# The mLSTM's gate columns inside the first group of memory queries

## The chip, the cores and the metric

The kernel runs on one core of a Trainium2 chip. The metric is the device time of one launch in microseconds, the median of several runs. One core has a matrix engine (TensorE, in the profile PE, its weight loads PEld), VectorE (DVE), ScalarE (ACT), GpSimd (POOL) and the sync engine (SP), which here only issues DMAs. Each works off its own queue of instructions in order. Products accumulate in eight PSUM banks.

## The reference

The reference is a decoder trunk of two layers for 256 tokens of width 1024. Each layer is a SwiGLU feed-forward half step, a token mixer beside memory cross-attention, and another half step. The change is in the first mixer, the mLSTM. One input matrix of 3592 columns serves all of it:

```python
proj = hn @ a_w_in[j]              # 256 tokens x 3592 columns
q, k  = tok[..., :512], tok[..., 512:1024]
v     = tok[..., 1024:2048]
o_gate = sigmoid(tok[..., 2048:3072])
gates = tok[..., 3072:3080] + gate_b
i_pre, logf = gates[..., :4], log_sigmoid(gates[..., 4:])
xq = proj[..., 3080:3592]          # memory queries, 4 heads of 128
q_mem = rms_norm(xq per head); softmax(q_mem k_mem^T / sqrt(128)) v_mem
```

`hn` is the RMS norm of the input. All is float32, and a product of float32 accuracy is made of three: each operand is split into a rounded part `h` and the rest `l`, and `h·h`, `h·l` and `l·h` are added up.

## The kernel before

Activations stand transposed: four tiles `xh` (rounded) and `xl` (rest), each 128 channels by 2 by 256 tokens. The RMS scale of a token is not applied to the input; it multiplies the results later, as a row `x.rb` (one value a token along the free axis) or as a column `x.rc` (one value a partition). Both come out of a chain that ends while the mixer's first products already run.

**Weights.** A `Stream` brings them from HBM in chunks, in a fixed `plan`. Each chunk passes a DMA into one of five `wr` buffers (`fetch`, sync queue), a rounding copy on ScalarE into `wh` (`round`) and a subtraction on VectorE into `wl` (`rest`). A chunk is copied at most `AHEAD = 5` chunks ahead of the one in use. A full chunk is 128 partitions by 4x256 and feeds 24 matmuls.

**Groups.** A `Group` is 256 output columns, two full chunks, 48 matmuls into one bank. In the usual form the weights are the stationary operand and the 256 tokens move, so the result has channels on partitions. With `rows=True` the activations are stationary and 256 weight columns move, so the result has tokens on partitions. `mm3` issues the three products; all matmuls of it are line 449 in the profile. Transposes are line 463, plain float32 products (`mmf`) line 458.

**The first mixer** (`mixer_a`) computes in this order: two groups of output gates, chunks alternating; the eight gate columns; two more groups of output gates; two groups of memory queries (`rows=True`); queries and keys; values; the output projection. The gate columns are a chunk of their own, 8x8 numbers a partition. They are spread over a tile of 128 columns, four at 0 and four at 32, after a memset of the rest on GpSimd (lines 299 and 311). Eight row chunks by three products give 24 matmuls that put the input gates on partitions 0 to 3 and the forget gates on 32 to 35 of `gate_bank`. `gates()` copies these rows out, multiplies them by `x.rb` and goes on with bias, exponential, logarithm and scans, writes a row to HBM and reads it back to all partitions.

**Consumers.** `out_gate` scales a group and, once the gates are done, applies a sigmoid (line 1025); the first loads ScalarE's sigmoid table, the last of four loads the table with exponential and logarithm again. `cross` takes a bank of memory queries through `head_norm` (squares on ScalarE, a reduction on VectorE, a power on GpSimd, a scaling), transposes the result (`turn`), and spawns two heads: scores, maximum, exponential (line 929), scaling, transposes, values.

**Order.** All instructions are put in order by a planner at build time, `Weave`. It has a clock of TensorE that grows with each matmul and a clock for each other engine, fed by estimated costs (`Job`). The main program yields every six matmuls or so; there the planner lets every chain run whose planned time has come, and fills the stream. Chains that put work on TensorE ask for `room`, a free bank.

Of the kernel before, what the change touches and what calls it, by code (L numbers as in the profile page):

```python
# [10 lines left out]
F32 = mybir.dt.float32  # L11
# [41 lines left out]
AHEAD = 5  # L53
LEAD = 0.4
NEAR = 2
HOP = 0.04
POLL = 0.6

# [54 lines left out]
class Job:  # L113
# [13 lines left out]
    def act(self, n=8, total=False):  # L127
        return self.use("act", 0.14 + n * 0.00092 + 0.09 * total)
# [12 lines left out]
def tile_trunk(ctx: ExitStack, tc: tile.TileContext, a, out):  # L141
# [3 lines left out]
    def mk(pool, shape, dt, tag):  # L145
        seq[0] += 1
        return pool.tile(shape, dt, tag=tag, name=f"{tag}_{seq[0]}")
# [121 lines left out]
    class Stream:  # L269
# [22 lines left out]

        def round(self, i):
            shape, j = self.plan[i][1], Job(wv, self.landed[i])
            gates = shape[2] == 8
            n = 1024 if gates else shape[1] * shape[2]
            self.hi[i] = mk(whp[i % 2], [P, 8, P] if gates else shape, F32R, f"wh{i % 2}")
            if gates:
                nc.gpsimd.memset(self.hi[i].bitcast(F32), 0.0)
                for s in range(2):  # L300
                    nc.scalar.copy(self.hi[i][:, :, s * 32:s * 32 + 4], self.raw[i][:, :, s * 4:s * 4 + 4])
            else:
                nc.scalar.copy(self.hi[i], self.raw[i])  # L303
            self.cast[i] = j.act(n)

        def rest(self, i):
            shape, j = self.plan[i][1], Job(wv, self.cast[i])
            gates = shape[2] == 8
            self.lo[i] = mk(wlp[i % 2], [P, 8, P] if gates else shape, F32R, f"wl{i % 2}")
            if gates:  # L310
                nc.gpsimd.memset(self.lo[i].bitcast(F32), 0.0)
                for s in range(2):
                    d = slice(s * 32, s * 32 + 4)
                    tt(out=self.lo[i][:, :, d], in0=self.raw[i][:, :, s * 4:s * 4 + 4],
                       in1=self.hi[i][:, :, d].bitcast(F32), op=ALU.subtract)
                j.dve(64)
            else:
                tt(out=self.lo[i], in0=self.raw[i], in1=self.hi[i].bitcast(F32), op=ALU.subtract)  # L318
                j.dve(shape[1] * shape[2])
            self.subbed[i] = j.t  # L320

        def fill(self):
# [42 lines left out]
    def chunks(w):  # L365
        return w.rearrange("(k p) f -> p k f", p=P)
# [54 lines left out]
    def mixer_plan(w, pair, rest, w_out, gates=None):  # L421
        for kh in range(2):
            for c0 in pair:
                yield cols(w, c0, kh)
        for c0 in rest:
            if c0 == gates:
                yield chunks(w)[:, :, c0:c0 + 8], [P, 8, 8], None
                continue
            for kh in range(2):
                yield cols(w, c0, kh)  # L430
        for kc in ORDER + LATE:
            yield row(w_out, kc)

    A_PAIR, A_REST = (2048, 2304), (3072, 2560, 2816, 3080, 3336, 0, 512, 256, 768, 1024, 1280, 1536, 1792)
    B_PAIR, B_REST = (1024, 1280), (1536, 0, 256, 512, 768)
    plan = list(mem_plan())
    for i, (src, shape, _) in enumerate(list(ffn_plan(a["ffn1_w_in"][0], a["ffn1_w_out"][0]))):
# [209 lines left out]

    def head_norm(j, dst, src, n, x, scales):

        hd = src.shape[2] // n  # L650
        sq, v, u = tmp(), col(), col()
        sqv = sq[:, :, :n * hd]
        act(sqv, src, AF.Square)
        yield j.act(2 * n * hd)
        nc.vector.tensor_reduce(out=v[:, 0:2 * n].rearrange("p (h m) -> p h m", h=2),
                                in_=sqv.rearrange("p h (m d) -> p h m d", m=n), axis=AX.X, op=ALU.add)
        j.dve(2 * n * hd)
        yield from x.wait(j)
        hsc = scales(j)
        for h in range(2):  # L660
            nc.vector.tensor_scalar(u[:, n * h:n * h + n], v[:, n * h:n * h + n], hsc[:, h:h + 1], EPS,
                                    op0=ALU.mult, op1=ALU.add)
            j.dve()
        power(j, u[:, 8:8 + 2 * n], u[:, 0:2 * n], 2 * n)
        yield j.t
        for h in range(2):
            nc.vector.tensor_scalar(v[:, 8 + n * h:8 + n * h + n], u[:, 8 + n * h:8 + n * h + n],
                                    hsc[:, 2 + h:3 + h], None, op0=ALU.mult)
            j.dve()
        tt(out=dst.rearrange("p h (m d) -> p h m d", m=n), in0=src.rearrange("p h (m d) -> p h m d", m=n),  # L670
           in1=v[:, 8:8 + 2 * n].rearrange("p (h m) -> p h m", h=2).unsqueeze(3).to_broadcast([P, 2, n, hd]),
           op=ALU.mult)
        j.dve(2 * n * hd)
# [227 lines left out]
        def has(self, *kcs):  # L901
            return lambda: all(kc in self.done for kc in kcs)

    def cross(gr, gi, layer, x, scales, ys):
        j = Job(wv)
        qn = unit(F32)
        yield from head_norm(j, qn, gr.ps, 2, x, scales)
        gr.b.free()
        yield from room(j, 1)
        b = turn(qn)  # L910
        yield j.pe()
# [96 lines left out]
    def mixer_a(x, nxt):  # L1008
# [26 lines left out]
                yield from gr.part(kh)  # L1035


        yield main_banks(1)
        gate_bank = Bank()
        yield ws.ready()  # L1040
        gh, gl = ws.take()
        for kc in range(8):
            mm3(gate_bank.t[:, :T], gh[:, kc], gl[:, kc], x.xh[kc // 2][:, kc % 2], x.xl[kc // 2][:, kc % 2],
                start=kc == 0, stop=kc == 7)
            if kc % 2 == 1:
                yield
        ws.drop()

        def gates():
            j, ps = Job(wv), gate_bank.t  # L1050
            yield from x.wait(j)
            gt = [unit(F32) for _ in range(4)]
            ipre, fpre, ab, bc, av, gg, em, one = (gt[i // 2][0:4, i % 2] for i in range(8))
            nc.vector.memset(one, 1.0)
            nc.scalar.copy(ipre, ps[0:4, :T])
            j.act(T)
            nc.scalar.copy(fpre, ps[32:36, :T])
            yield j.act(T)
            gate_bank.free()
            tt(out=ipre, in0=ipre, in1=x.rb[0:4], op=ALU.mult)  # L1060
            tt(out=fpre, in0=fpre, in1=x.rb[0:4], op=ALU.mult)
            nc.vector.tensor_scalar(ipre, ipre, gbias[:, 0:1], None, op0=ALU.add)
            nc.vector.tensor_scalar(fpre, fpre, gbias[:, 1:2], None, op0=ALU.add)
            stt(out=ab, in0=fpre, scalar=-1.0, in1=fpre, op0=ALU.mult, op1=ALU.max)
            for _ in range(6):
                j.dve(T)
            yield j.t
            act(ab, ab, AF.Exp, scale=-1.0)
            j.act(T)
            act(ab, ab, AF.Ln, bias=1.0)  # L1070
            yield j.act(T)
            stt(out=fpre, in0=fpre, scalar=0.0, in1=ab, op0=ALU.min, op1=ALU.subtract)
            nc.vector.tensor_tensor_scan(bc, one, fpre, 0.0, ALU.mult, ALU.add)
            tt(out=av, in0=ipre, in1=bc, op=ALU.subtract)
            nc.vector.tensor_tensor_scan(gg, one, av, 0.0, ALU.mult, ALU.max)
            tt(out=em, in0=bc, in1=gg, op=ALU.add)
            for _ in range(7):
                j.dve(T)
            yield j.t
            gd = a["gd"]  # L1080
            nc.gpsimd.dma_start(gd, gg)
            gb = [unit(F32) for _ in range(2)]
            for i in range(2):
                nc.gpsimd.dma_start(gb[i], gd[2 * i:2 * i + 2, :].partition_broadcast(P))
            st["gb"], st["at"] = gb, j.t + 9.0
            act(em, em, AF.Exp, scale=-1.0)
            st["gates"] = j.act(T)
            acol = mk(gp, [P, 16], F32, "acol")
            yield from room(j, 1)
            b = Bank()  # L1090
            for i, r in enumerate((av, em)):
                for h in range(2):
                    transpose(b.t[:, (2 * i + h) * 4:(2 * i + h) * 4 + 4], r[:, h * P:(h + 1) * P])
            yield j.pe()
            nc.vector.tensor_copy(acol, b.t[:, :16])
            j.dve()
            b.free()
            st["acol"], st["at"] = acol, max(st["at"], j.t)

        wv.spawn(gates())  # L1100
        for i, gr in enumerate(gs):
            wv.spawn(out_gate(i, gr))
        for i in range(2, 4):
# [1 line left out]
            gr = Group(x)  # L1105
            yield from gr.all()
            wv.spawn(out_gate(i, gr))
        hsc = head_scales(x, P, True)
        for gi in range(2):
            yield main_banks(1)  # L1110
            gr = Group(x, rows=True)
            yield from gr.all()
            wv.spawn(cross(gr, gi, 0, x, hsc, ys))

        def decay(hd):
            j = Job(wv)
# [188 lines left out]
    def mixer_b(x, nxt):  # L1305
# [130 lines left out]
            for gr in (g0, g1):  # L1436
                yield from gr.part(kh)
        wv.spawn(keys(g0))
        wv.spawn(cross(g1, 0, 1, x, hsx, ys))
        yield main_banks(1)  # L1440
        gr = Group(x, rows=True)
        yield from gr.all()
        wv.spawn(cross(gr, 1, 1, x, hsx, ys))
        for gi in range(4):
            yield main_banks(1)
            gr = Group(x, rows=True)
# [55 lines left out]
```

## Time and profile before

| | |
|---|---|
| median of 3 runs | 1001.41 us (1001.22 to 1002.0) |
| the profiled execution's own time | 1001.35 us |
| its span, first to last instruction | 999.6 us |
| instructions | 20574 |
| TensorE matmuls | 8554 |
| DMA, mean | 183 GB/s |

In the profile's groups a row names line, engine and operation, then what is written and read, the moving operand first (`bank<-xh,wh`: the activations move, the weights stand; `bank<-wh,xh`: the other way round). "x1544" is a count, then come busy time, mean duration of one and idle time before. Matmuls overlap in the pipeline: one is shown as some 280 ns long, but the next starts much sooner, so prices are read from the distance of their starts. In the chain of waits a piece is a stretch of one line's work, with start, length and count.

### The profile page before, as it was taken

To read this page: it belongs to the slowest core of one execution; us is meant where nothing else is said; L and a number is where in the kernel's file an instruction comes from. 1 tells how busy PE (TensorE), PEld (TensorE's weight loads), DVE (VectorE), ACT (ScalarE), POOL (GpSimd) and SP (SyncE) were. 2 spreads that over 40 slices of the span, in tenths; PEclk is the share of its full clock that TensorE was granted. 3 is DMA by queue.
4 is the path that set the end of the run, shared out by engine and by line. 5 is a ranking of instruction groups with operands and counts; after the bars stand their busy time and mean duration, and the time that the engine had idled before them with its cause. 6 is when DMAs were issued, how large, how long until landed. Compare 5 with 4: busy or idle time off the path is not lost.

```text
span 999.6 us, 20574 instructions
## 1 busy us (share of the span) xinstructions
PE 991.2 (99%) x8554; PEld 976.6 (98%) x8554; DVE 677.3 (68%) x1096; ACT 511.0 (51%) x774; POOL 56.7 (6%) x46
## 2 busy tenths in 40 slices
PE   8999999999999999999999999999999999999998
PEld 7999999999999999999999999999998899999997
DVE  6985675578767596666568676656678788665561
ACT  6754444356656464454454544444566765544440
POOL 1400000011001000000010000001122010000000
PEclk9999999999999999999999999999999999999999
DMA  9876656666354566655676557565623357666550
GB/s 298 246 236 208 190 168 195 208 170 201 114 172 134 183 211 203 210 180 173 197 216 195 190 170 225 187 197 174 189 85 101 98 163 252 189 193 211 187 169 23
DMA packets 171613, 182.71 MB, mean 183 GB/s; under 512 B 7196, under 2 KB 165328, under 8 KB 171520
## 3 DMA queue, kind: packets, MB, share of 16 engines
q1 hardware_dynamic: 170384, 179.60, 57.7%
q8 instruction: 67, 1.10, 0.4%
q0 software_dynamic: 416, 0.75, 0.4%
q10 hardware_dynamic: 720, 1.05, 0.3%
q14 instruction: 26, 0.21, 0.1%
HBM read 180.32 MB, written 1.05 MB: 181 GB/s over the span
## 4 chain that ended last, share of the span: by engine, by line
PE 98%; DMA 1%; ACT 0%; DVE 0%; issue 0%; SPq 0%; DVEq 0%; ACTq 0%
PE bank L449 93%; PE bank L458 2%; PE bank L463 2%; DMA wr<-in_mem_w_kv_dram 1%; PE bank L1374 1%; PE bank L1425 1%; PE bank L1369 0%; DMA u<-in_memT_dram 0%; ACT wh L303 0%; ACT u L709 0%; DVE wl L318 0%; DVE t L868 0%; DVE t L869 0%; SPq L379 0%; DVE u L711 0%
## 5 line engine op out<-in xcount | busy, mean ns | idle before, releaser
L318 DVE TENSOR_TENSOR wl<-wr,wh 128x1024 fp32r<-128x1024 f32 (+2 forms) x349 | 407.0, 1204 | 51.9 <-ACT wh L303 50.5
L449 PE MATMUL bank<-xh,wh 128*128 128x256 f32 x1544 | 427.4, 277 | 0.0
L449 PE MATMUL bank<-xh,wl 128*128 128x256 f32 x1544 | 426.4, 276 | 0.0
L449 PE MATMUL bank<-xl,wh 128*128 128x256 f32 x1544 | 426.4, 276 | 0.0
L303 ACT CAST wh<-wr 128x1024 fp32r<-128x1024 f32 (+2 forms) x349 | 339.0, 1019 | 74.4 <-PE bank L449 48.9
L449 PE MATMUL bank<-u,wh 128*128 128x256 f32 x1792 | 307.9, 277 | 0.0
L449 PEld LDWEIGHTS bank<-xh,wh 128*128 128x128 f32 x1544 | 289.8, 188 | 0.1
L449 PEld LDWEIGHTS bank<-xl,wh 128*128 128x128 f32 x1544 | 289.8, 188 | 0.1
L449 PEld LDWEIGHTS bank<-xh,wl 128*128 128x128 f32 x1544 | 289.8, 188 | 0.0
L449 PEld LDWEIGHTS bank<-u,wh 128*128 128x128 f32 x1792 | 269.8, 188 | 1.7 <-issue 1.7
L449 PE MATMUL bank<-u,wl 128*128 128x256 f32 x896 | 247.5, 276 | 0.0
L449 PEld LDWEIGHTS bank<-u,wl 128*128 128x128 f32 x896 | 168.2, 188 | 0.0
L800 ACT ACTIVATE t<-t 128x512 f32<-128x512 f32 x44 | 27.9, 633 | 185.9 <-DVE t L797 185.5
L797 DVE TENSOR_TENSOR t<-bank,rb 128x256 f32<-128x256 f32 x88 | 36.5, 422 | 77.2 <-PE bank L449 77.2
L449 PE MATMUL bank<-wh,xh 128*128 128x256 f32 x208 | 60.1, 289 | 0.0
L449 PE MATMUL bank<-wl,xh 128*128 128x256 f32 x208 | 58.1, 279 | 0.0
L449 PE MATMUL bank<-wh,xl 128*128 128x256 f32 x208 | 58.0, 279 | 0.0
L497 ACT ACTIVATE xh<-u,gcol 128x256 fp32r<-128x256 f32 x48 | 21.6, 501 | 71.2 <-DVE u L850 58.6
L523 POOL TENSOR_TENSOR u<-u,t 128x512 f32<-128x512 f32 x14 | 24.3, 1736 | 592.5 <-ACT t L520 592.4
L847 DVE TENSOR_TENSOR t<-bank,hrb 128x512 f32<-128x512 f32 x15 | 10.4, 691 | 62.1 <-PE bank L449 62.1
L803 DVE TENSOR_TENSOR t<-t,bank 128x256 f32<-128x256 f32 x88 | 33.0, 417 | 27.0 <-ACT t L800 26.9
L469 DVE TENSOR_TENSOR u<-t,u 128x512 fp32r<-128x512 f32 x44 | 30.4, 691 | 28.2 <-ACT u L467 28.2
(189 smaller groups left out, 658.9 us busy)
## 6 DMA issues: line engine op xcount, KB each, us to landing
wr<-in_ffn_w_in_dram SPq DMA_DIRECT2D x176, 512.0 KB, 5.2
wr<-in_ffn_w_out_dram SPq DMA_DIRECT2D x80, 512.0 KB, 4.9
wr<-in_a_w_in_dram SPq DMA_DIRECT2D x28, 512.0 KB, 4.7
wr<-in_b_w_in_dram SPq DMA_DIRECT2D x14, 512.0 KB, 4.7
wr<-in_a_w_out_dram SPq DMA_DIRECT2D x12, 512.0 KB, 3.9
wr<-in_b_w_out_dram SPq DMA_DIRECT2D x12, 512.0 KB, 3.3
wr<-in_ffn_w_out_dram SPq DMA_DIRECT2D x16, 256.0 KB, 2.8
wr<-in_mem_w_kv_dram SPq DMA_DIRECT2D x6, 512.0 KB, 7.6
```

The costliest lines, as they stand in the source:

```text
L303: nc.scalar.copy(self.hi[i], self.raw[i])
L318: tt(out=self.lo[i], in0=self.raw[i], in1=self.hi[i].bitcast(F32), op=ALU.subtract)
L449: nc.tensor.matmul(ps, lhsT, rhs, start=start, stop=stop, skip_group_check=True)
L458: nc.tensor.matmul(ps, lhsT, rhs, start=start, stop=stop, skip_group_check=True)
L463: nc.tensor.transpose(ps, src, ident[:k, :k])
L469: tt(out=lo, in0=src, in1=hi.bitcast(F32), op=ALU.subtract)
L497: act(hi[:, m], xn[:, m], AF.Copy, scale=g(self.gi + 2 * c2 + m))
L523: nc.gpsimd.tensor_tensor(out=self.acc, in0=self.acc, in1=sq, op=ALU.add)
L797: tt(out=t[:, m], in0=bs[m].t[:, :T], in1=x.rb, op=ALU.mult)
L800: act(t, t, AF.Silu)
L803: tt(out=t[:, m], in0=t[:, m], in1=bs[m].t[:, T:], op=ALU.mult)
L847: tt(out=t, in0=halves(b.t), in1=pair(x.hrb), op=ALU.mult)
```

## The change

The eight gate columns lie next to the first 256 columns of the memory queries in the input matrix. They are now one stretch of 264 columns. Its chunks are 2 row chunks by 264 columns, four of them, and the group is placed where the gates stood, behind the first two groups of output gates. It has the rows' form, one bank for each half of the tokens: 48 matmuls of 264 moving columns. The gates come out with tokens on partitions. `gates()` copies their eight columns of each half out, scaled by `x.rc`, into a zeroed tile of 36 columns (four at 0, four at 32), and two transposes bring them into the old layout; the multiplications by `x.rb` are gone. The memory queries are the columns 8 to 263 of both banks. `head_norm` and `cross` take a list of two such views, and work on the halves one after the other. The second query group follows the output gates as before, and so do all others.

```diff
+GATED = 264
...
         def round(self, i):
             shape, j = self.plan[i][1], Job(wv, self.landed[i])
-            gates = shape[2] == 8
-            n = 1024 if gates else shape[1] * shape[2]
-            self.hi[i] = mk(whp[i % 2], [P, 8, P] if gates else shape, F32R, f"wh{i % 2}")
-            if gates:
-                nc.gpsimd.memset(self.hi[i].bitcast(F32), 0.0)
-                for s in range(2):
-                    nc.scalar.copy(self.hi[i][:, :, s * 32:s * 32 + 4], self.raw[i][:, :, s * 4:s * 4 + 4])
-            else:
-                nc.scalar.copy(self.hi[i], self.raw[i])
-            self.cast[i] = j.act(n)
+            self.hi[i] = self.split(whp[i % 2], f"wh{i % 2}", shape)
+            nc.scalar.copy(self.hi[i], self.raw[i])
+            self.cast[i] = j.act(shape[1] * shape[2])
+
+        def split(self, pool, tag, shape):
+            if shape[2] == GATED:
+                return mk(pool, [P, shape[1], 384], F32R, tag)[:, :, :GATED]
+            return mk(pool, shape, F32R, tag)
...
             if c0 == gates:
-                yield chunks(w)[:, :, c0:c0 + 8], [P, 8, 8], None
+                for k in range(0, 8, 2):
+                    yield chunks(w)[:, k:k + 2, c0:c0 + GATED], [P, 2, GATED], None
                 continue
...
-    A_PAIR, A_REST = (2048, 2304), (3072, 2560, 2816, 3080, 3336, 0, 512, 256, 768, 1024, 1280, 1536, 1792)
+    A_PAIR, A_REST = (2048, 2304), (3072, 2560, 2816, 3336, 0, 512, 256, 768, 1024, 1280, 1536, 1792)
...
-        yield main_banks(1)
-        gate_bank = Bank()
-        yield ws.ready()
-        gh, gl = ws.take()
-        for kc in range(8):
-            mm3(gate_bank.t[:, :T], gh[:, kc], gl[:, kc], x.xh[kc // 2][:, kc % 2], x.xl[kc // 2][:, kc % 2],
-                start=kc == 0, stop=kc == 7)
-            if kc % 2 == 1:
-                yield
-        ws.drop()
+        hsc = head_scales(x, P, True)
+        yield main_banks(2)
+        gbs = [Bank(), Bank()]
+        for k0 in range(0, 8, 2):
+            yield ws.ready()
+            wh, wl = ws.take()
+            for m in range(2):
+                ms = slice(m * P, (m + 1) * P)
+                for k in range(2):
+                    kc = k0 + k
+                    mm3(gbs[m].t[:, :GATED], x.xh[kc // 2][:, kc % 2, ms], x.xl[kc // 2][:, kc % 2, ms],
+                        wh[:, k], wl[:, k], start=kc == 0, stop=kc == 7)
+                if m == 0:
+                    yield
+            ws.drop()
+            yield
 
         def gates():
...
+            rows = unit(F32)[:, :, :36]
+            nc.gpsimd.memset(rows, 0.0)
+            for h in range(2):
+                act(rows[:, h].rearrange("p (s c) -> p s c", c=4)[:, 0:9:8],
+                    gbs[h].t[:, :8].rearrange("p (s c) -> p s c", s=2), AF.Copy, scale=x.rc[:, h:h + 1])
+                j.act()
+            st["read"] = True
+            yield from room(j, 1)
+            b = Bank()
+            for h in range(2):
+                transpose(b.t[:36, h * P:(h + 1) * P], rows[:, h])
+            yield j.pe()
...
-            tt(out=ipre, in0=ipre, in1=x.rb[0:4], op=ALU.mult)
-            tt(out=fpre, in0=fpre, in1=x.rb[0:4], op=ALU.mult)
...
+        def first_queries():
+            while "read" not in st:
+                yield wv.now + POLL
+            yield from cross([b.t[:, 8:GATED] for b in gbs], gbs, 0, 0, x, hsc, ys)
+
         wv.spawn(gates())
+        wv.spawn(first_queries())
         for i, gr in enumerate(gs):
             wv.spawn(out_gate(i, gr))
...
-        hsc = head_scales(x, P, True)
-        for gi in range(2):
-            yield main_banks(1)
-            gr = Group(x, rows=True)
-            yield from gr.all()
-            wv.spawn(cross(gr, gi, 0, x, hsc, ys))
+        yield main_banks(1)
+        gr = Group(x, rows=True)
+        yield from gr.all()
+        wv.spawn(cross(gr.ps, [gr.b], 1, 0, x, hsc, ys))
```

More of the change, by code (lines that the diff above doesn't have):

```diff
@@ L294, in round @@
             shape, j = self.plan[i][1], Job(wv, self.landed[i])
-            gates = shape[2] == 8
-            n = 1024 if gates else shape[1] * shape[2]
-            self.hi[i] = mk(whp[i % 2], [P, 8, P] if gates else shape, F32R, f"wh{i % 2}")
-            if gates:
-                nc.gpsimd.memset(self.hi[i].bitcast(F32), 0.0)
-                for s in range(2):
-                    nc.scalar.copy(self.hi[i][:, :, s * 32:s * 32 + 4], self.raw[i][:, :, s * 4:s * 4 + 4])
-            else:
-                nc.scalar.copy(self.hi[i], self.raw[i])
-            self.cast[i] = j.act(n)
+            self.hi[i] = self.split(whp[i % 2], f"wh{i % 2}", shape)
[5 more added lines that the diff above has]
+            return mk(pool, shape, F32R, tag)
         def rest(self, i):
             shape, j = self.plan[i][1], Job(wv, self.cast[i])
[L308 to L319, printed above, removed]
+            self.lo[i] = self.split(wlp[i % 2], f"wl{i % 2}", shape)
+            tt(out=self.lo[i], in0=self.raw[i], in1=self.hi[i].bitcast(F32), op=ALU.subtract)
+            j.dve(shape[1] * shape[2])
             self.subbed[i] = j.t
@@ L648, in head_norm @@
     def head_norm(j, dst, src, n, x, scales):
-        hd = src.shape[2] // n
+        hd = dst.shape[2] // n
         sq, v, u = tmp(), col(), col()
         sqv = sq[:, :, :n * hd]
-        act(sqv, src, AF.Square)
-        yield j.act(2 * n * hd)
+        if isinstance(src, list):
+            for h in range(2):
+                act(sqv[:, h], src[h], AF.Square)
+                j.act(n * hd)
+        else:
+            act(sqv, src, AF.Square)
+            j.act(2 * n * hd)
+        yield j.t
         nc.vector.tensor_reduce(out=v[:, 0:2 * n].rearrange("p (h m) -> p h m", h=2),
@@ L669, in head_norm @@
             j.dve()
+        if isinstance(src, list):
+            for h in range(2):
+                tt(out=dst[:, h].rearrange("p (m d) -> p m d", m=n), in0=src[h].rearrange("p (m d) -> p m d", m=n),
+                   in1=v[:, 8 + n * h:8 + n * (h + 1)].unsqueeze(2).to_broadcast([P, n, hd]), op=ALU.mult)
+                j.dve(n * hd)
+            return
         tt(out=dst.rearrange("p h (m d) -> p h m d", m=n), in0=src.rearrange("p h (m d) -> p h m d", m=n),
@@ L902, in has, with cross @@
             return lambda: all(kc in self.done for kc in kcs)
-    def cross(gr, gi, layer, x, scales, ys):
+    def cross(src, banks, gi, layer, x, scales, ys):
         j = Job(wv)
         qn = unit(F32)
-        yield from head_norm(j, qn, gr.ps, 2, x, scales)
-        gr.b.free()
+        yield from head_norm(j, qn, src, 2, x, scales)
+        for b in banks:
+            b.free()
         yield from room(j, 1)
@@ L1035, in mixer_a @@
                 yield from gr.part(kh)
-        yield main_banks(1)
-        gate_bank = Bank()
-        yield ws.ready()
-        gh, gl = ws.take()
-        for kc in range(8):
-            mm3(gate_bank.t[:, :T], gh[:, kc], gl[:, kc], x.xh[kc // 2][:, kc % 2], x.xl[kc // 2][:, kc % 2],
-                start=kc == 0, stop=kc == 7)
-            if kc % 2 == 1:
-                yield
-        ws.drop()
+        hsc = head_scales(x, P, True)
[14 more added lines that the diff above has]
+            yield
         def gates():
-            j, ps = Job(wv), gate_bank.t
+            j = Job(wv)
             yield from x.wait(j)
+            rows = unit(F32)[:, :, :36]
+            nc.gpsimd.memset(rows, 0.0)
+            for h in range(2):
+                act(rows[:, h].rearrange("p (s c) -> p s c", c=4)[:, 0:9:8],
[4 more added lines that the diff above has]
+            b = Bank()
+            for h in range(2):
+                transpose(b.t[:36, h * P:(h + 1) * P], rows[:, h])
+            yield j.pe()
             gt = [unit(F32) for _ in range(4)]
@@ L1054, in gates @@
             nc.vector.memset(one, 1.0)
-            nc.scalar.copy(ipre, ps[0:4, :T])
+            nc.scalar.copy(ipre, b.t[0:4, :T])
             j.act(T)
-            nc.scalar.copy(fpre, ps[32:36, :T])
+            nc.scalar.copy(fpre, b.t[32:36, :T])
             yield j.act(T)
-            gate_bank.free()
-            tt(out=ipre, in0=ipre, in1=x.rb[0:4], op=ALU.mult)
-            tt(out=fpre, in0=fpre, in1=x.rb[0:4], op=ALU.mult)
+            b.free()
             nc.vector.tensor_scalar(ipre, ipre, gbias[:, 0:1], None, op0=ALU.add)
@@ L1064, in gates @@
             stt(out=ab, in0=fpre, scalar=-1.0, in1=fpre, op0=ALU.mult, op1=ALU.max)
-            for _ in range(6):
+            for _ in range(4):
                 j.dve(T)
@@ L1438, in mixer_b @@
         wv.spawn(keys(g0))
-        wv.spawn(cross(g1, 0, 1, x, hsx, ys))
+        wv.spawn(cross(g1.ps, [g1.b], 0, 1, x, hsx, ys))
         yield main_banks(1)
@@ L1442, in mixer_b @@
         yield from gr.all()
-        wv.spawn(cross(gr, 1, 1, x, hsx, ys))
+        wv.spawn(cross(gr.ps, [gr.b], 1, 1, x, hsx, ys))
         for gi in range(4):
```

## The prediction

> **What bounds the kernel now.** I read the page first: busy shares, the chain that ended last, the costliest groups.
>
> ```profile
> span 999.6 us, 20574 instructions
> ## 1 busy us (share of the span) xinstructions
> PE 991.2 (99%) x8554; PEld 976.6 (98%) x8554; DVE 677.3 (68%) x1096; ACT 511.0 (51%) x774; POOL 56.7 (6%) x46
> ...
> PE 98%; DMA 1%; ACT 0%; DVE 0%; issue 0%; SPq 0%; DVEq 0%; ACTq 0%
> ...
> L449 PE MATMUL bank<-xh,wl 128*128 128x256 f32 x1544 | 426.4, 276 | 0.0
> ```
>
> TensorE is busy 99% of the span, 98% of the chain is its own work, and the large product groups have 0.0 us of idle time before them. A busy engine need not be at its best pace, so I next read the chain as single pieces over the first mixer. Each row is a run of matmuls of one line: its end marks, its length, its count.
>
> ```profile
> 204.98 31.28 PE bank L449 x276
> 236.59 15.03 PE bank L449 x126
> 251.62 0.44 PE bank L463 x4
> 252.06 2.06 PE bank L449 x18
> 254.12 1.73 PE bank L458 x8
> ...
> 275.58 10.30 PE bank L449 x90
> ...
> 291.44 1.30 PE bank L458 x6
> ...
> 307.43 5.65 PE bank L449 x48
> ```
>
> Three prices come out of it. An undisturbed fp32r product of 256 columns costs 31.28/276 = 113.3 ns. A 128x128 transpose costs 0.44/4 = 110 ns (109 in the records). A plain fp32 pass of 256 columns (L458) costs 1.73/8 = 216 ns, and of 257 columns 1.30/6 = 217 ns. And there is a second pace of the fp32r products: 48 of them take 5.65 us, 117.7 ns each. The run from 236.59 has it as well, (15.03 − 0.1 of restart)/126, about 118.5 ns. Such slow stretches begin behind plain fp32 work or transposes, and they end again: 90 in 10.30 us is 114.4 ns, 18 in 2.06 us is 114.4 ns.
>
> Last the timeline of TensorE around the gates' small transposes and the start of the memory queries.
>
> ```profile
> 235.98 0.28 PE L449 MATMUL bank<-xh,wl 128*128 128x256 f32 x1
> 236.19 0.41 PE L463 MATMUL bank<-con,u 4*128 4x4 f32 x4
> 236.52 0.38 PE L449 MATMUL bank<-xh,wh 128*128 128x256 f32 x1
> 236.74 0.28 PE L449 MATMUL bank<-xl,wh 128*128 128x256 f32 x1
> ...
> 238.74 0.28 PE L449 MATMUL bank<-wh,xh 128*128 128x256 f32 x1
> ```
>
> From the matmul at 235.98 to the one at 236.74 pass 0.76 us. Two fp32r products would take 0.23, so four tiny transposes cost 0.53. At 238.74 the rows' form of the products begins, the weights moving. That is the first group of memory queries, 48 products, to 238.74 + 48 × 0.118 = 244.4. Counted back from 238.74 over 96 products of the output gates and the 0.53, the padded gate group lies at 224.5 to 227.2, inside the 276 that run without a break.
>
> **What the change removes.** The padded group is 24 matmuls (eight row chunks, three products each), each a full 256 columns for eight useful rows. All lie on the path: 24 × 113.3 = 2.72 us gone. The two POOL memsets that padded it go too:
>
> ```profile
> 206.74 0.96 POOL L299 MEMSET wh<- 128x1024 f32 x1 [2.35 <-PE bank L449]
> 207.63 0.96 POOL L311 MEMSET wl<- 128x1024 f32 x1
> ```
>
> They stand 16 us ahead of the products that need them, so they are worth nothing in time. The two multiplications of the gates by the row scale on VectorE go as well; they are off the path.
>
> **What it adds on TensorE.** (1) Eight columns on 48 products. No row shows 264 columns of fp32r. Below: nothing, if the pace is set by something other than the columns. Above, within a smooth price: 113.3/256 × 8 = 3.5 ns, 0.17 us in all. Plain fp32 is linear where it can be read: 128 columns 110 ns, 256 columns 216, 257 columns 217, so 0.83 ns a column at two cycles; half of it is 0.41 ns, and 8 × 0.41 × 48 = 0.16 us. I take 0.16, since that row differs only in the type.
>
> The Trainium skill, "TensorE: Matmul & The Clock Gate", section "Back-to-back issue gap", states N/2.4 + 2.5 ns for a warm stream: 109.2 ns at 256 and 112.5 at 264. The trace has 113.3 at 256, so the page's figure is already under the measured pace; if something else holds that pace, 264 columns fit below it, and the sum would be 0.16 us better than mine.
>
> (2) Two transposes of 128 tokens by 36 columns. Below: 2 × 109 = 0.22 us, from the 128x128 row. Above: half of the 0.53 of the tiny ones, 0.27. I take 0.23, since in size they are like the former.
>
> (3) The pace. The first query group now stands ahead of any transpose, in the 113.3 pace, where it stood in the slow one: 48 × 4.5 ns = 0.22 less. In exchange the new transposes come in the first output-gate chunk behind it, and up to 84 products of the two output-gate groups may fall into the slow pace: up to 0.38 more, and nearly nothing if the pace comes back within a few matmuls as at 252.06. I take 0.22 for it, so the two cancel, and keep ±0.2 as a bound.
>
> **What it moves, and who covers it.** The weights of this stretch arrive as four chunks of 2x264 in place of one tiny and two full ones. Copy, subtraction and transfer are the same amount of data (1056 bytes a row where there were 1024), in one more issue on the sync queue. What changes is the look-ahead: it is counted in chunks, five of them, and four are now 12 products long, 1.4 us. In the worst place the copy of a full chunk may start four halves and a full one ahead, 4 × 1.4 + 2.7 = 8.3 us. What it needs:
>
> ```profile
> wr<-in_a_w_in_dram SPq DMA_DIRECT2D x28, 512.0 KB, 4.7
> ```
>
> ```profile
> 236.72 2.35 DVE L318 TENSOR_TENSOR wl<-wr,wh 128x1024 fp32r<-128x1024 f32 x2
> ```
>
> The transfer is issued before that, as soon as the fifth chunk before it has left its buffer. The worst subtraction now is the first of these two, done at about 237.9 for products that start at 244.4: 6.5 us in hand, while VectorE works off the gates. Subtractions are put off for such work, but queued at the latest when the chunk two before is taken up. Two halves are 2.8 us, a subtraction 1.2, so the floor of the cover is 1.6 us of VectorE's queue; it holds since the gates' chain on VectorE only starts when the halves are used up. If it went, TensorE would wait by what is missing, up to the 1.2 us of a subtraction.
>
> The gates' rows are now copied out on ScalarE (eight columns, twice), transposed on TensorE and copied again. The transposes wait for ScalarE, and behind them on TensorE stand the output-gate products, for which the rest of the kernel waits. The order by hand puts them at the first break past the planned end of the copies, one break being six products, 0.68 us; I count no stall, with 0.5 us as its price. The memset of the rows is POOL's and has no other work ahead of it. The first queries' chain (squares, reduction, power on POOL, scaling, transposes, two heads) runs 14 us sooner. Its power is queued on POOL when the squares are queued, ahead of the gates' transfers there, so it isn't held by them. The later groups (queries, keys, values) start their chains from their own products and move with TensorE.
>
> **The sum.** −2.72 + 0.16 + 0.23 + 0 = −2.33 us. The profiled execution took 1001.35, of which 999.6 is the span; so 999.02. The median shown, 1001.41, is 0.06 above it: 999.1. With the bounds (−2.72 + 0.22 + 0 − 0.2 and −2.72 + 0.27 + 0.17 + 0.2) and some 0.3 us between runs this case reaches from 998.5 to 999.6. A difference of 0.2%, 2.0 us, is about what a measurement of this kernel can tell from no change, so this case sits just beyond it.
>
> **Rival 1: function tables.** ScalarE loads a table where the functions change:
>
> ```profile
> 234.97 1.28 ACT L180 ACT_TABLE_LOAD   x1
> ...
> 239.70 0.64 ACT L1025 ACTIVATE u<-u 128x512 f32<-128x512 f32 x1 [0.81 <-DVE u L1017]
> 240.36 1.28 ACT L180 ACT_TABLE_LOAD   x1
> ...
> 244.63 0.60 ACT L653 ACTIVATE t<-bank 128x512 f32<-128x512 f32 x1
> ...
> 255.77 0.47 ACT L929 ACTIVATE u<-bank,col 128x256 f32<-128x256 f32 x1 [2.04 <-DVE col L926]
> ```
>
> Today the sigmoids (L1025) lie between two loads, and the first exponentials of the memory heads (L929) come 14 us after the second. With the change the first query group ends at 224.5 + 48 × 0.1166 = 230.1, and its exponentials follow about 11.4 us behind (255.77 − 244.4), near 241.5. The first sigmoid load moves to about 239 (7.8 us behind the end of the gates' products, as now, and a copy and a transpose more), and the last sigmoid to 241.0 + 1.0 = 242.0, as the two output-gate groups end at 241.0. So the exponentials may well fall between sigmoids: two more loads, 2.57 us of ScalarE that the planned order doesn't count. ScalarE has room on the whole, but the heads' transposes on TensorE have their fixed place:
>
> ```profile
> 258.61 0.69 DVE L936 TENSOR_TENSOR u<-u,col 128x512 f32<-128x512 f32 x1
> ```
>
> ```profile
> 259.96 1.04 PE L463 MATMUL bank<-con,u 128*128 128x128 f32 x8
> ```
>
> Their input is ready at 259.30, 0.66 us ahead. One late load costs TensorE 1.28 − 0.66 = 0.6 us, two 2.57 − 0.66 = 1.9 us: 999.6 to 1001.0. The interleaving is as likely as not; that TensorE feels it is less so, since a load that comes while ScalarE waits anyway is free. Chance 0.20.
>
> The Trainium skill, "ScalarE: Activation LUTs", section "Table sets: the hidden batching unit", has the rule that speaks against this change: do all activations of one table set before those of the next. It puts a switch at about 2.7 us with its drain, where the row has 1.28 us for the load; by that figure the two switches would give back 4.7 us at most.
>
> **Rival 2, slower: 264 columns fall out of the fast pace.** If fp32r products of this length run as plain fp32 passes do, each costs 216 × 264/256 = 223 ns in place of 116.6: 48 × 0.106 = 5.1 us more, 1004.1. It breaks even at 116.6 + 2.33/48 = 165 ns a product. The step from 256 to 257 columns costs plain fp32 1 ns, which speaks against a cliff; nothing in this trace shows fp32r beyond 256. Chance 0.08.
>
> **Rival 3: no gain.** Something behind the mixer's TensorE work is late anyway, and the 2.3 us come back as a wait ahead of the output projection: 1001.4. Against it: the chain shows no such wait today, and those chains start from products that move by the same amount. Chance 0.06.
>
> **How the numbers follow.** The forecast has 0.62, of which 0.56 lies past the 2.0 us. Rival 1, rival 3 and the near end of the forecast make "same" 0.34. Slower is rival 2 and 0.02 for what I don't see (a buffer that comes free late): 0.10. The range from 998.5 to 1001.0 takes in the forecast and rival 1, and leaves out rivals 2 and 3 and a little more.
>
> **What would show it.** Right: 8532 matmuls (24 fewer, 2 more); no memset in the weights' tiles; 264-column products at 113 to 117 ns; TensorE without idle time in this stretch; the pieces of the chain from 205 to 330 shorter by 2.3 us and nothing given back after. Wrong: 264-column products at over 165 ns; two table loads more, and a wait of TensorE on the heads' transposes; idle time ahead of the output projection; a chunk's first product waiting for its subtraction.

## The result and the profile after

The changed kernel is slower: 1003.18 us (22 runs, 1001.5 to 1005.24) against 1001.26 us for the kernel before (22 runs, 999.31 to 1002.55). The ratio is 1.0024, 95% interval 1.0018 to 1.0029. The profiled execution took 1002.53 us.

The page after, the same lines as before:

```profile
span 1000.7 us, 20536 instructions
## 1 busy us (share of the span) xinstructions
PE 987.6 (99%) x8532; PEld 972.3 (97%) x8532; DVE 676.2 (68%) x1095; ACT 516.3 (52%) x781; POOL 54.5 (5%) x45
...
PE 95%; ACT 2%; DMA 1%; DVE 1%; issue 0%; POOL 0%; SPq 0%; ACTq 0%; DVEq 0%
```

The 22 matmuls fewer are there, and TensorE is busy 3.6 us less. But its share of the chain fell from 98% to 95%, and ScalarE stands in the chain with 2%. "99% busy" is the same number in both kernels; the chain is where the difference shows.

The two spans don't compare directly: the first product of the mixer comes at 213.43 before and at 211.75 after, in code that the change doesn't touch. The granted clock of the first 40 us was 0.96 in the one trace and 1.00 in the other, and likewise the runs of most kernels fall into two groups by their mean granted clock, 1.4 to 2.3 us apart (the kernel before, beside e1: medians 1000.31 at 0.999 or more and 1002.14 below), so that a median depends on how many of each it has. So I measure from that product to the first one of the next feed-forward. Before:

```profile
213.43 0.28 PE L449 MATMUL bank<-xh,wh 128*128 128x256 f32 x1
...
346.43 0.28 PE L449 MATMUL bank<-xh,wh 128*128 128x256 f32 x1
```

After:

```profile
211.75 0.28 PE L441 MATMUL bank<-xh,wh 128*128 128x256 f32 x1
...
347.97 0.28 PE L441 MATMUL bank<-xh,wh 128*128 128x256 f32 x1
```

The mixer, so measured, took 133.0 us and takes 136.2: 3.2 us more where 2.3 less was forecast. What TensorE waited for in that stretch (us in total, times, longest), after the change; before, the list is empty here:

```profile
PE bank L455 <- DVE u L943: 2.7, 1, 2.7
PE bank L455 <- ACT u L1069: 1.0, 1, 1.0
PE bank L450 <- ACT t L952: 0.7, 1, 0.7
```

The chain of the same stretch, in order of time, names what was behind each:

```profile
222.98 1.89 ACT wh L297 x2
224.87 5.09 DMA wr<-in_a_w_in_dram
230.21 0.80 issue
231.01 0.42 ACT u L1069 x2
...
238.55 1.28 ACT L181
239.84 0.63 ACT u L1032
240.49 1.28 ACT L936
241.79 1.02 ACT u L936 x4
242.83 1.28 ACT L1032
244.12 1.15 ACT u L1032 x2
245.29 1.28 ACT L936
246.59 1.02 ACT u L936 x4
247.61 0.48 ACT t L952
248.09 0.95 ACT wh L297
249.05 1.28 ACT L1032
250.34 0.64 ACT u L1032
251.00 1.28 ACT L181
```

L936 is the heads' exponential, L1032 the output gates' sigmoid, and a row without a tile on their lines is a table load. Two heads and four sigmoids alternate, and four loads (240.49, 242.83, 245.29, 249.05) lie between the two that the code asks for. Behind them come the heads' transposes and values, for which TensorE waits 2.7 and 0.7 us. On TensorE's timeline the starts lie 2.96 and 0.96 us apart there, where those of two products lie 0.12 apart:

```profile
245.72 0.28 PE L441 MATMUL bank<-wh,xl 128*128 128x256 f32 x1
248.68 0.41 PE L455 MATMUL bank<-con,u 128*128 128x128 f32 x2 [2.68 <-DVE u L943]
...
251.97 0.28 PE L441 MATMUL bank<-wh,xl 128*128 128x256 f32 x1
252.93 0.70 PE L450 MATMUL bank<-t,vM 128*128 128x256 f32 x2 [0.68 <-ACT t L952]
```

The third wait, 1.0 us for the gates' rows (L1069), goes back to a transfer. On ScalarE's timeline:

```profile
227.04 1.05 ACT L297 CAST wh<-wr 128x1024 fp32r<-128x1024 f32 x1 [1.13 <-DMA wr<-in_a_w_in_dram]
230.06 1.04 ACT L297 CAST wh<-wr 128x1024 fp32r<-128x1024 f32 x1 [1.96 <-DMA wr<-in_a_w_in_dram]
231.01 0.42 ACT L1069 ACTIVATE u<-bank,rc 128x8 f32<-128x8 f32 x2
```

A weight copy is queued ahead of the gates' reads. It waits 1.96 us for its transfer, and the reads, whose products ended at 228.9, wait behind it. TensorE in turn holds the transposes ahead of the output-gate products, and 1.30 us pass from the start of the product before them to theirs:

```profile
230.02 0.28 PE L441 MATMUL bank<-xh,wl 128*128 128x256 f32 x1
231.32 0.45 PE L455 MATMUL bank<-con,u 128*36 128x128 f32 x2 [1.02 <-ACT u L1069]
```

### The profile page after: what moved, and what is told of

Same layout as the page of the kernel before. It is cut to its first block, busy times and chain, and to the rows that moved or that the text cites. A ratio compares the mean times of both kernels' runs of the same rounds, so it can differ in the third digit from the quotient of the medians.

```text
span 1000.7 us, 20536 instructions
## 1 busy us (share of the span) xinstructions
PE 987.6 (99%) x8532; PEld 972.3 (97%) x8532; DVE 676.2 (68%) x1095; ACT 516.3 (52%) x781; POOL 54.5 (5%) x45
## 4 chain that ended last, share of the span: by engine, by line
PE 95%; ACT 2%; DMA 1%; DVE 1%; issue 0%; POOL 0%; SPq 0%; ACTq 0%; DVEq 0%
PE bank L441 90%; PE bank L450 2%; PE bank L455 1%; DMA wr<-in_mem_w_kv_dram 1%; PE bank L1402 1%; PE bank L1453 1%; DMA wr<-in_a_w_in_dram 1%; ACT wh L297 0%; PE bank L1397 0%; ACT L181 0%; ACT L1032 0%; ACT L936 0%; DMA u<-in_memT_dram 0%; ACT u L1032 0%; ACT u L936 0%
## 5 line engine op out<-in xcount | busy, mean ns | idle before, releaser
L309 DVE TENSOR_TENSOR wl<-wr,wh 128x1024 fp32r<-128x1024 f32 (+3 forms) x351 | 405.9, 1195 | 51.7 <-ACT wh L297 50.5
L297 ACT CAST wh<-wr 128x1024 fp32r<-128x1024 f32 (+3 forms) x351 | 339.9, 1015 | 84.7 <-PE bank L441 46.9
L441 PE MATMUL bank<-wh,xh 128*128 128x256 f32 (+1 forms) x208 | 60.6, 291 | 0.0
L441 PE MATMUL bank<-wl,xh 128*128 128x256 f32 (+1 forms) x208 | 58.1, 279 | 0.0
L441 PE MATMUL bank<-wh,xl 128*128 128x256 f32 (+1 forms) x208 | 58.0, 279 | 0.0
```

The source lines that it names most:

```text
L441: nc.tensor.matmul(ps, lhsT, rhs, start=start, stop=stop, skip_group_check=True)
```

## The experiments

Theory 1: the group's new place lets exponentials fall between sigmoids; the planner doesn't know of the loads, so it places the heads' work on TensorE too early. Theory 2: the gates' reads stand behind a weight copy that is queued before its data has landed. The rival is that the 264-column products, or ScalarE's lost time as such, carry the loss.

| kernel | median us | ratio to the kernel before, 95% | mixer us | waits of TensorE listed there, us | below the kernel before, medians of the runs at a clock of 0.999 or more, us |
|---|---|---|---|---|---|
| changed | 1003.18 | 1.0024 (1.0018 to 1.0029) | 136.2 | 2.7, 1.0, 0.7 | not on record |
| e1_hold | 999.76 | 0.9987 (0.9978 to 0.9996) | 132.5 | 0.7 | 1.6 |
| e2_counted | 998.79 | 0.9981 (0.9972 to 0.9989) | 131.9 | 0.3 | 1.6 |
| e3_read_dve | 1000.27 | 0.9995 (0.9986 to 1.0004) | 133.0 | 1.4 in two | 0.9 |
| e4_hold_read | 998.06 | 0.9977 (0.9967 to 0.9986) | 131.3 | none | 2.3 |
| e5_order_only | 1002.27 | 1.0019 (1.0009 to 1.0028) | 134.5 | 1.1 | −1.0 |
| e7_256 | 999.04 | 0.9985 (0.9976 to 0.9994) | 131.0 | none | 2.4 |
| e8_two_chunks | 998.45 | 0.9983 (0.9974 to 0.9992) | 130.9 | none | 1.9 |
| e9_behind_read | 999.18 | 0.9985 (0.9976 to 0.9994) | 131.4 | none | 2.7 |
| e10_two_chunks_read | 997.60 | 0.9976 (0.9964 to 0.9987) | 131.2 | none | 2.3 |
| e11_order_hold | 999.86 | 0.9998 (0.9989 to 1.0007) | 132.9 | none | 0.3 |

The ratios and the last column go against runs of the kernel before that were taken beside each one. The mixer column is from one profile each; the kernel before has 133.0 there.

**Heads behind the sigmoids (e1_hold).**

```diff
+            self.hold = lambda: False
...
         def head(m):
             hd, j = gi * 2 + m, Job(wv)
+            while ys.hold():
+                yield max(j.t, wv.now + POLL)
...
+        ys.hold = lambda: len(og) < 4
```

> The changed kernel, with one wait in the plan: the memory heads of the first mixer start only when all four sigmoids are queued. Its ScalarE order then has no table load inside the sigmoids (three loads in the mixer, as before the change). Theory 1 (TensorE waits because the order on TensorE was planned without the four extra loads): the waits of 2.9 and 0.8 us ahead of the heads' transposes and values go, 1.2 us ahead of the gates' transposes stays; about 3.6 us less than the changed kernel, 999.6, some 1.7 us below the kernel before. Rival (the 264-column products or their slower pace carry the loss): within 0.4 us of the changed kernel, 1003.

The loads between the sigmoids are gone and so are both waits behind them; the mixer is 3.7 us shorter than in the changed kernel, as theory 1 wants. One wait is left, the gates', 0.7 us.

**The loads kept, but counted (e2_counted).**

```diff
         wv.clock["act"] += 1.3
+        wv.tab = name
+
+    def switch(name):
+        if wv.tab != name:
+            wv.clock["act"] += 1.3
+            wv.tab = name
...
+            switch("natural_log_exp_and_others")
...
+            switch("sigmoid_and_others")
```

The first of the two calls stands ahead of a head's exponentials, the second ahead of a sigmoid.

> The changed kernel, with the planner's ScalarE clock advanced by 1.3 us at each switch between sigmoid and exponential. The four extra loads stay, 5.1 us of ScalarE, in the same order. Theory 1 (it is the plan, not ScalarE's lost time): TensorE gets other work ahead of the heads' transposes and waits less than 0.6 us there in place of 3.6; about 1000.0. Rival (ScalarE's time itself is what is short): TensorE still waits 3 us or more, only elsewhere; 1003.

ScalarE does the same four extra loads, in nearly the same order, and they last as long:

```profile
242.39 1.28 ACT L943 ACT_TABLE_LOAD   x1
...
244.72 1.28 ACT L1040 ACT_TABLE_LOAD   x1
...
247.18 1.28 ACT L943 ACT_TABLE_LOAD   x1
...
249.51 1.28 ACT L1040 ACT_TABLE_LOAD   x1
...
252.75 0.59 ACT L959 COPY t<-bank 128x512 f32<-128x512 f32 x1
```

And TensorE doesn't feel them. The copy at 252.75 ends at 253.34, and its reader on TensorE now stands at 254.73, behind other products:

```profile
254.73 1.03 PE L456 MATMUL bank<-t,vM 128*128 128x256 f32 x4
```

Its list of waits holds the gates' row alone (0.3 us). So ScalarE's 5.1 us aren't the price; that the order on TensorE was made without them is. This run was better than expected, and better than e1 by 0.6 us in the mixer, 0.4 of it in the gates' wait.

**Gate columns read by VectorE (e3_read_dve).**

```diff
-                act(rows[:, h]..., gbs[h].t[:, :8]..., AF.Copy, scale=x.rc[:, h:h + 1])
-                j.act()
+                nc.vector.tensor_scalar(rows[:, h]..., gbs[h].t[:, :8]..., x.rc[:, h:h + 1], None, op0=ALU.mult)
+                j.dve()
```

> The changed kernel, with the eight gate columns read by VectorE in place of ScalarE. Theory 2 (the reads stood on ScalarE behind a weight copy that waited for its transfer): the wait of 1.2 us ahead of the gates' transposes goes. The planner's order moves a little with it: two extra table loads in place of four, so up to half of the 3.6 us of the heads' waits may go as well: 1000.2 to 1002.0. Rival (the transposes wait for the products of the bank themselves, or for the memset): the 1.2 us stay in the trace.

The gates' wait is gone, which is theory 2's sign. The order moved with it, as was expected, and only two loads between the sigmoids remain (244.72 and 247.53), and with them two waits for the copies behind them, 1.4 us.

**Both (e4_hold_read).** The two edits together.

> Both edits together: heads behind the sigmoids, gate columns read by VectorE. Theories 1 and 2 together: no wait of TensorE over 0.3 us in the first mixer, 4.8 us less than the changed kernel, 998.4, some 2.8 us below the kernel before, which is the gain that was forecast and a little more. If a new wait takes the place of the old ones: 1000 or more.

No wait is listed. The weight copy still waits 1.66 us for its transfer, but the gates' reads no longer stand behind it. The mixer takes 131.3 us, 1.7 below the kernel before, in time 0.9977.

**The order alone (e5_order_only), and with the hold (e11_order_hold).** The kernel before, gates padded as they were, with the first query group moved in the weights' plan and, not shown, in the mixer's code; e11 has the hold of e1 as well:

```diff
-    A_PAIR, A_REST = (2048, 2304), (3072, 2560, 2816, 3080, 3336, 0, ...)
+    A_PAIR, A_REST = (2048, 2304), (3072, 3080, 2560, 2816, 3336, 0, ...)
```

> The kernel before, with one thing moved: the first group of memory queries ahead of the last two groups of output gates. The padded gate group stays, there are no 264 columns and no new transposes. Its ScalarE order has two table loads inside the sigmoids. Theory 1 (the order of the groups, not the merging, brings the loads and the heads' waits): TensorE waits for 0.5 to 2 us in the heads, 1001.9 to 1003.4, slower than the kernel before. Rival (merging is what loses, moving costs nothing): within 0.3 us of the kernel before.

> The kernel before, with the first query group moved ahead of the last two output-gate groups and the heads held until all four sigmoids are queued. Theory 1 (the moved order loses by the table loads alone): no wait of TensorE over 0.3 us, the same time as the kernel before within 0.4 us, first mixer 133.0 us. Rival (the moved order costs in another way as well, say in the slow pace of the products): 0.5 us or more slower than the kernel before.

The move without the merging loses 1.5 us in the mixer, and the profile has the same sign: two loads more (242.62 and 249.23) than in the kernel before. The second delays the last sigmoid and the load behind it (251.18, which the code asks for), and TensorE waits 1.1 us for the copy that follows:

```profile
249.23 1.28 ACT L1025 ACT_TABLE_LOAD   x1
250.53 0.63 ACT L1025 ACTIVATE u<-u 128x512 f32<-128x512 f32 x1
251.18 1.28 ACT L180 ACT_TABLE_LOAD   x1
252.47 0.58 ACT L945 COPY t<-bank 128x512 f32<-128x512 f32 x1
```

With the hold the loss is gone (132.9 against 133.0). So the new place costs nothing once the loads are kept out, and what e4 and e8 gain is the merging's.

**Eight columns less (e7_256).** e4 with the products at 256 columns; the last eight of the 264 are left out, so the queries are not the right ones.

```diff
-   mm3(gbs[m].t[:, :GATED], ..., wh[:, k], wl[:, k], ...)
+   mm3(gbs[m].t[:, :T], ..., wh[:, k, :T], wl[:, k, :T], ...)
```

> Heads behind the sigmoids and gate columns read by VectorE, but the 48 merged products move 256 columns in place of 264 (the last eight of the 264 are left out, and the queries are taken from column 0). The 264-column products took 122.1 ns in every run so far. If eight columns cost 3.4 ns and the rest is the slow pace, these take 117.8; if the length itself takes them out of the fast pace, these take 113.4, 0.42 us less, and the output-gate products behind them start at 113.3 in place of 117.9, another 0.1 to 0.3 us. Time 997.3 to 998.0.

In the changed kernel the 48 products run from 222.86 to 228.72, in e7 from 225.36 to 230.97:

```profile
222.86 0.29 PE L441 MATMUL bank<-wh,xh 128*128 128x264 f32 x1
...
228.60 0.28 PE L441 MATMUL bank<-wh,xl 128*128 128x264 f32 x1
228.72 0.28 PE L441 MATMUL bank<-xh,wh 128*128 128x256 f32 x1
```

```profile
225.36 0.28 PE L441 MATMUL bank<-wh,xh 128*128 128x256 f32 x1
...
230.97 0.28 PE L441 MATMUL bank<-xh,wh 128*128 128x256 f32 x1
```

That is 122.1 ns and 116.9 ns a product on average. Of the 8.8 ns between 122.1 and the 113.3 of an undisturbed product, 5.2 go with the eight columns, 0.25 us in all, where 3.4 were counted. The other 3.6 are the slow pace, which this group has at 256 columns too: its starts lie 117 to 119 ns apart, for a stretch in the middle 113 to 115, although no transpose or plain fp32 work stands in the 25 us ahead of it. So the slow pace was no matter of the length, and the second alternative of the expectation fell. The median, 999.04, lies above the 997.3 to 998.0 that were expected; the mixer, 131.0 us against 131.3 in e4, fits the 0.25.

**Two long chunks (e8_two_chunks).** e1 with the weights in two chunks of 4x264, reads on ScalarE as in the change (the tiles lose their padding to 384 columns, and the planner's breaks stay at every six products):

```diff
-                for k in range(0, 8, 2):
-                    yield chunks(w)[:, k:k + 2, c0:c0 + GATED], [P, 2, GATED], None
+                for k in range(0, 8, 4):
+                    yield chunks(w)[:, k:k + 4, c0:c0 + GATED], [P, 4, GATED], None
```

> Heads behind the sigmoids, gate columns read by ScalarE as in the change, but the merged weights come as two chunks of 4x264 in place of four of 2x264 (tiles without the padding to 384). Theory 2 (four short chunks use up a look-ahead that is counted in chunks, so a weight copy is queued on ScalarE ahead of its transfer and the gates' reads wait behind it): the copy no longer waits for its transfer there, and the wait of 1.0 us ahead of the gates' transposes goes; 998.5. Rival (ScalarE is behind by itself at that place): the wait stays at 0.7 us or more, 999.5.

No copy waits for a transfer there any more, and each read starts when its own products end:

```profile
226.00 1.98 ACT L297 CAST wh<-wr 128x1024 fp32r<-128x1024 f32 x2
229.81 0.27 ACT L1073 ACTIVATE u<-bank,rc 128x8 f32<-128x8 f32 x1 [1.83 <-PE bank L441]
231.24 0.27 ACT L1073 ACTIVATE u<-bank,rc 128x8 f32<-128x8 f32 x1 [1.16 <-PE bank L441]
```

The gates' wait went without touching the reads, so its first cause is the short chunks. The mixer takes 130.9 us, 2.1 below the kernel before. Against e1 that is 1.6 less, more than the wait of 0.7 that went; the rest was not taken apart.

**The merged group behind all output gates (e9_behind_read).** The gate reads are on VectorE, and the group is moved in the plan and, not shown, in the mixer's code:

```diff
-    A_PAIR, A_REST = (2048, 2304), (3072, 2560, 2816, 3336, 0, ...)
+    A_PAIR, A_REST = (2048, 2304), (2560, 2816, 3072, 3336, 0, ...)
```

> The change with the merged group moved behind all four groups of output gates, so that the four sigmoids stand together without any hold, and the gate columns read by VectorE. Theory 1: no table load inside the sigmoids and no wait of TensorE over 0.3 us in the heads; 998 to 998.5. If the later gates hold up the decay of queries and keys, a new wait ahead of those products: 999.5 or more.

There are no loads between sigmoids and no waits, and the mixer takes 131.4 us. The median, 999.18, is above what was expected, but the last column has the largest gain of all, 2.7 us, so the median doesn't speak against this order. The profile shows nothing that the later gates hold up.

**All three mends (e10_two_chunks_read).**

> All three mends of the change: heads behind the sigmoids, gate columns read by VectorE, two chunks of 4x264. If each wait has one cause and the two mends of the gates' wait do the same thing, it is no better than two chunks with the hold alone: first mixer 130.9 us, 998.4, some 1.9 us below the kernel before. If reading on VectorE still brings the gates forward: up to 0.4 us less.

The mixer takes 131.2 us, no better than e8, as it should be with two cures of the same wait. In time e4, e8 and e10 (0.9977, 0.9983, 0.9976) can't be told apart; all beat both kernels, the one before by about 0.2%.

## Why the prediction was wrong

Two steps failed: the price of rival 1, the table loads, and the wait of the gates' transposes, which was put at nothing. What the change removes was right.

- **The 24 matmuls** went, and most of what they are worth came out. In the runs with the merging and no listed wait (e4, e8, e9, e10) the mixer is 1.6 to 2.1 us shorter than before; the forecast without its error on the long products (below) was 2.33 − 0.26 = 2.1. What keeps three of them up to 0.5 us from it is open.
- **The 264 columns.** Their step was mis-sized: 0.16 us counted on top of 113.3 ns, 122.1 ns measured, 48 × (122.1 − 116.6) = 0.26 us more. By e7's average, 0.09 of it are the columns and 0.17 the slow pace. Rival 2, a fall to 223 ns, did not happen. The formula of the Trainium skill, "TensorE: Matmul & The Clock Gate", "Back-to-back issue gap", would give 112.5 ns, which isn't met either; the prediction applied it to a stream, while that section gives it for a single matmul and has other figures for a stream of weight loads and products.
- **The pace** (step 3 of the additions) was argued from a wrong rule: the slow pace began with the group itself, not with the transposes behind it, so the 0.22 us that the group was to gain did not come.
- **Rival 1** is what came, and its price was too low. I wrote "two more loads", 1.9 us at the most and 0.20 as the chance. The trace has four loads, and TensorE's waits behind them show as start distances of 2.96 and 0.96 us where a product takes 0.12: 3.7 us. In e1, without the loads, the mixer is 3.7 us shorter, 0.3 of it by the gates' wait. The price left out that a second sigmoid could come between the two heads, and that later work stands behind later loads. The chance was too low because I took ScalarE's free time as cover: it covers the loads in e2, where the planner counts them and places the readers later, and not here, where the readers' place on TensorE was fixed without them.
- **"I count no stall, with 0.5 us as its price"**, on the gates' transposes, failed: 1.30 us from the last product to the transposes, 1.2 lost. I had looked for a late subtraction as what short chunks could cost; it was a copy queued too early, with the reads behind it. The row that I quoted for the transfers, 4.7 us, was the one to hold against the planner's estimate, 2.9 us for 512 KB in an idle queue (1.4 + 1.5 in its code); this transfer stands in the chain with 5.09.
- **The sum.** −2.33 + 3.7 + 1.2 + 0.26 = +2.8 of the 3.2 us measured; the remaining 0.4 was not taken apart; the pace of other products and the restarts behind the waits are candidates, not shown.
- **The rule against the change.** The Trainium skill, "ScalarE: Activation LUTs", "Table sets: the hidden batching unit", has the rule that pointed at this: all of one set before the next. The trace agrees in direction, though e2, which switches as often, has no wait behind its loads, so the switches harm by the order that was planned without them. With its figure, 2.7 us a switch, the trace does not agree: in the chain of the changed kernel a sigmoid ends at 240.47, the load runs from 240.49 for 1.28 us and the exponential starts at 241.79, 1.32 us for the switch.

## What to carry to other kernels

When a step is moved, list what the engines' hidden state (here ScalarE's table) is at the old and at the new place, and count a switch for each alternation. In an order fixed at build time, an estimate that misses 1.3 us can cost the engine that sets the time, however much free time the other engine has: give the planner the switch, or hold the one kind behind the other. A look-ahead counted in chunks shrinks when the chunks do, and a copy that is queued before its data lands blocks everything behind it on its engine.

## What the runs showed of the hardware

The split products have two paces. In the rows' form with 256 columns 48 of them took 116.9 ns each on average in e7, without transposes or plain fp32 work in the 25 us ahead of them, where the same form runs at 113.3 ns in one group of values before the change (24 products from 283.00 to 285.72). What sets the pace stays open. In the changed kernel's chain a table load started 0.02 us after the end of the activation ahead of it (240.47 to 240.49), took 1.28 us, and the next activation started 0.02 us behind it.
